# Split weights that move past the transposed input begin 32 bytes into their buffers

## The chip, the cores and the metric

The kernel runs on one core of a Trainium2 chip. Its time is device microseconds of that core for one execution of the whole program; lower is better. TensorE multiplies matrices: one operand of 128 columns is loaded into the array (LDWEIGHTS, the stationary operand) and up to 512 columns of the other move past it (MATMUL). VectorE and ScalarE do elementwise work, GpSimd (POOL) a little, and SyncE (SP) issues the transfers from device memory.

## The reference

A decoder trunk of two layers on a sequence of 256 tokens, model width 1024, all in float32. Each layer is a half-step SwiGLU FFN (inner width 2816), a token-mixing sub-layer, and a second FFN; a final norm follows.

```python
for l in range(DEPTH):
    h = h + 0.5 * swiglu(rms_norm(h, ffn1_norm[l]), ffn1_w_in[l], ffn1_w_out[l])
    u = rms_norm(h, mix_norm[l])
    (z_s, xbc, dt_s, qkv, z_d, b_d, a_d, gate_s, gate_d) = jnp.split(u @ w_in[l], split_points, axis=-1)
    y_s = mamba2_branch(z_s, xbc, dt_s, ...)
    y_d = deltanet_branch(qkv, z_d, b_d, a_d, ...)
    merged = (jax.nn.sigmoid(gate_s) * (y_s @ ssm_w_branch[l])
              + jax.nn.sigmoid(gate_d) * (y_d @ dn_w_branch[l]))
    h = h + merged @ w_out[l]
    h = h + 0.5 * swiglu(rms_norm(h, ffn2_norm[l]), ffn2_w_in[l], ffn2_w_out[l])
return rms_norm(h, final_norm)
```

## The kernel before

A float32 product is made of three products of a shorter format (fp32r): each operand is split into a high part and a low rest, and hi·hi, hi·lo and lo·hi are added in PSUM. The weights come from memory in forms of 128 x 1024 float32 (4096 bytes in each partition), in the order in which they are used. A list, `plan`, holds one entry for each form: its kind, which raw loads it needs, and how many loads must have been issued. `take()` hands out the next form; ahead of it, `load` issues transfers into five buffers `wraw`, and `prep` has ScalarE write the high part (`whi`) and VectorE the rest (`wlo`), into a ring of five buffers each (`NSPL`). Most forms have kind "d"; the kinds "q0" to "q6" are those of a block scheme in the second FFN product, which are also added and subtracted before they are split.

The normalised input is turned by TensorE, split in the same way, and kept in one tile `uT` (high and low part, 8 blocks of 128 input rows, 256 tokens). In the layout of the memory within a partition, `h` (8192 bytes), `cs` (3584), `mhalf` (4, padded to 32), `one` (512) and two tiles `Y` (2048 each) precede `uT`, and it begins at byte 32928, which is 257 x 128 + 32. The ten buffers of `whi` and `wlo` begin at byte 78464 = 613 x 128 and follow each other every 4096 bytes, so each begins on a multiple of 128, as do the tiles `gh`, `gl`, `bh`, `bl`, `mh`, `ml`, `bsa` to `bsd` (split activations) and `wsc`.

Which operand moves differs by place:
- `tok_chunk` (by way of `mm3`): a block of `uT` is stationary and 512 columns of `whi` or `wlo` move. It makes the first chunk of each FFN (PSUM tiles f) and, in the mixer, the z columns and the two gates (PSUM tiles t): 48 matmuls of 512 columns for a chunk of four forms, four chunks f and sixteen chunks t in all.
- `chan_pair` (PSUM tiles fc, the rest of the FFN's first product) and `chan_chunk` (kk, qq, vv, zd, bc, xs in the mixer): a block of the weights is stationary and `uT` moves.
- `out_chunks` and `block_products` (b, o, p): split activations are stationary and the weights move; `uT` isn't used.

In the mixer the string `ORDER` gives the order of the steps: z.. and g.. are token chunks (each name is half a chunk, two forms), k, q, v, d, b, x are channel chunks (two forms), N is the DeltaNet branch product (eight forms); the SSD branch product (16 forms) and the output product (8) follow. A scheduler (Tile) places the instructions of each engine and gives tiles of a pool their buffers in turn; `s2` is a pool of nine buffers of 2048 bytes for short-lived tiles.

Of the kernel before, what the change touches and what calls it, by code (L numbers as in the profile page):

```python
# [7 lines left out]
F32 = mybir.dt.float32  # L8
F32R = mybir.dt.float32r
# [7 lines left out]
P = 128  # L17
# [13 lines left out]
NSPL = 5  # L31
# [12 lines left out]
ORDER = """  # L44
# [7 lines left out]
def trunk_kernel(ctx, tc, x, wst, wsm, norms, lpar, rpar, cst, out):  # L52
# [4 lines left out]
    wpool = ctx.enter_context(tc.tile_pool(name="wpool", bufs=1))  # L57
    slots = ctx.enter_context(tc.tile_pool(name="slots", bufs=1))
    s2 = ctx.enter_context(tc.tile_pool(name="s2", bufs=9))
# [5 lines left out]
    def act(o, i, func=AF.Copy, **kw):  # L65
        return A.activation(out=o, in_=i, func=func, **kw)  # L66

    def tt(o, a, b, op):
        return V.tensor_tensor(out=o, in0=a, in1=b, op=op)  # L69

    def stt(o, a, s, b, op0, op1):
        return V.scalar_tensor_tensor(out=o, in0=a, scalar=s, in1=b, op0=op0, op1=op1)

    def ts(o, a, s1, op0, sc2=None, op1=None):
        if op1 is None:
            return V.tensor_scalar(out=o, in0=a, scalar1=s1, scalar2=None, op0=op0)
        return V.tensor_scalar(out=o, in0=a, scalar1=s1, scalar2=sc2, op0=op0, op1=op1)

    def f(ap):
        return ap.bitcast(F32)  # L80

    def tmp2(name):
        return s2.tile([P, 512], F32, tag="s2", name=name)

    def trb(name):
        return trp.tile([P, 512], F32, tag="tr", name=name)
# [4 lines left out]
    def small(shape, name, bufs=2):  # L91
        return sm.tile(shape, F32, tag=name, name=name, bufs=bufs)
# [3 lines left out]
    mix = (n_dram - 2 * DEPTH * (4 * FC + 22)) // DEPTH  # L96
    plan, stream = [], []

    def plan_plain(j, n):
        for i in range(j, j + n):  # L100
            stream.append(i)
            plan.append(("d", [len(stream) - 1], len(stream)))
        return j + n

    def plan_ffn(j):


        o, j2, held = j + 4 * FC, j + 4 * FC + 22, []
        for kind in FFN:
            if kind in "fc":  # L110
                j = plan_plain(j, 4 if kind == "f" else 2)
            elif kind == "d":
                o = plan_plain(o, 1)
            else:
                if kind == "A":
                    where = [len(stream) + i for i in range(3)]
                    stream.extend(range(o, o + 3))
                    held.append((where, o + 2))
                    o += 4
                    for i, need in enumerate((2, 3, 3, 3)):  # L120
                        plan.append((f"q{i}", where, where[0] + need))
                else:
                    where, b22 = held.pop(0)
                    where += [len(stream) + 1, len(stream)]
                    stream.extend([b22, b22 + 1])
                    for i in range(4, 7):
                        plan.append((f"q{i}", where, len(stream)))
        return j2

    j0 = 0  # L130
    for _ in range(DEPTH):
        j0 = plan_ffn(plan_plain(plan_ffn(j0), mix))
    assert j0 == n_dram
    n_raw = len(stream)
    first = {js[0] for kind, js, _ in plan if kind == "q0"}
# [12 lines left out]

    def prep(i):
        kind, js, _ = plan[i]  # L150
        hi = wpool.tile([P, 1024], F32R, tag="whi", name="whi", bufs=NSPL)
        lo = wpool.tile([P, 1024], F32R, tag="wlo", name="wlo", bufs=NSPL)

        def less(o, a, b):
            tt(raws[js[o]][:], raws[js[a]][:], raws[js[b]][:], ALU.subtract)


        r = raws[js[{"q2": 1, "q4": 4, "q5": 3}.get(kind, 0)]]
        with ExitStack() as behind:
            for ins in state["behind"].pop(i, ()):  # L160
                behind.enter_context(tc.issue_after(ins))
            act(hi[:], r[:])
            if kind == "q1":
                less(1, 2, 1)
            elif kind == "q2":
                less(0, 2, 0)
            elif kind == "q4":
                less(0, 3, 0)
            tt(lo[:], r[:], f(hi[:]), ALU.subtract)
            if kind == "q0":  # L170
                less(0, 1, 0)
        for o in {"d": (0,), "q2": (1,), "q3": (2,), "q4": (4,), "q5": (3,), "q6": (0,)}.get(kind, ()):
            raws.pop(js[o])
        halves[i] = (hi, lo)

# [360 lines left out]
    def mixer(l, nxt):  # L536
# [58 lines left out]
        def scalars():  # L595
            psm = trb("psm")
            for kt in range(KT):
                both = wsc[:, kt].rearrange("p o c -> p (o c)")
                if kt < KT - 1:
                    PE.matmul(psm[0:96, 0:S], both, uTh[:, kt, :], start=kt == 0, stop=False)  # L600
                PE.matmul(psm[0:48, 0:S], wsc[:, kt, 0], uTl[:, kt, :], start=False, stop=False)
                if kt == KT - 1:
                    PE.matmul(psm[0:96, 0:S], both, uTh[:, kt, :], start=False, stop=True)
            smT = s2.tile([96, S], F32, tag="s2", name="smT")
            act(smT[:], psm[0:96, 0:S])
            pst = trb("pst")
            for t in range(2):
                PE.transpose(pst[:, t * 96 : (t + 1) * 96], smT[:, t * P : (t + 1) * P], ident[0:96, 0:96])
            pv2 = pst[:, 0:192].rearrange("p (t o c) -> p t o c", t=2, o=2)
            pvs = small([P, 2, 48], "pvs", 1)  # L610
            pv = pvs[:]
            act(pv, pv2[:, :, 1])
            tt(pv, pv2[:, :, 0], pv, ALU.add)
            scr = s2.tile([P, 5, 2, 40], F32, tag="s2", name="scr")
            xb, ax, z, s_, q_ = (scr[:, i] for i in range(5))
            tt(xb, pv[:, :, 0:40], rp[:, None, 0:40].to_broadcast([P, 2, 40]), ALU.add)
            act(dq[:, :, 8:16], pv[:, :, 40:48], AF.Tanh, scale=0.5)
            ts(dq[:, :, 8:16], dq[:, :, 8:16], 0.5, ALU.mult, 0.5, ALU.add)
            ea = small([P, 40], "ea", 1)
            with tc.issue_after(state["input"][0].ins):  # L620
                act(ea[:], alog, AF.Exp)
            stt(ax, xb, -1.0, xb, ALU.mult, ALU.max)
            act(z, ax, AF.Exp, scale=-1.0)
            ts(s_, z, 2.0, ALU.add)
            V.reciprocal(out=s_, in_=s_)
            tt(s_, s_, z, ALU.mult)
            tt(q_, s_, s_, ALU.mult)
            ts(z, q_, 1.0 / 15.0, ALU.mult)
            for d_ in (13.0, 11.0, 9.0, 7.0, 5.0, 3.0):
                stt(z, z, 1.0 / d_, q_, ALU.add, ALU.mult)  # L630
            stt(z, z, 1.0, s_, ALU.add, ALU.mult)
            ts(ax, xb, 0.0, ALU.max)
            stt(sp[:], z, 2.0, ax, ALU.mult, ALU.add)
            stt(la[:], sp[:], -1.0, ea[:, None, :].to_broadcast([P, 2, 40]), ALU.mult, ALU.mult)
            yield
            psr = trb("psr")
            for t in range(2):
                PE.matmul(psr[0:40, t * 256 : (t + 1) * 256], la[:, t, :], UU, start=True, stop=True)
            pr = psr[:].rearrange("p (t c) -> p t c", t=2)
            V.tensor_copy(rows[0:32], pr[0:32, :, 0:P])  # L640
            V.tensor_copy(rows[32:40], pr[32:40, :, P : 2 * P])
            nc.sync.dma_start(rdram[:], rows[:].rearrange("p t c -> p (t c)"))
            pac = trb("pac")
            for t in range(2):
                PE.transpose(pac[:, t * 40 : (t + 1) * 40], rows[:, t, :], ident[0:40, 0:40])
            V.tensor_copy(ac[:], pac[:, 0:80].rearrange("p (t c) -> p t c", t=2))
            V.tensor_copy(dq[:, :, 0:8], ac[:, :, 32:40])
            yield
            psp = trb("psp")
            for c in range(4):  # L650
                PE.matmul(psp[:, c * 16 : (c + 1) * 16], SEL[c % 2], dq[:, c // 2, :], start=True, stop=True)
            for a in range(2):
                V.tensor_copy(
                    pq[64 * a : 64 * a + 64].rearrange("p k h c -> p c k h"),
                    psp[64 * a : 64 * a + 64, 0:64].rearrange("p (c k h a) -> p c k h a", c=4, k=2, h=4)[:, :, :, :, a],
                )
# [484 lines left out]
        def dn_branch():  # L1141
            ps = branch("d", 4, dn_T)
            m = tg[1]
            for t in range(2):
                for n in range(2):
                    sl = slice(n * 512, (n + 1) * 512)
                    stt(m[:, t, sl], m[:, t, sl], 1.0, ps[t][n][:], ALU.add, ALU.mult)

        sc, inv, rc = scalars(), invert(), recur()
        units = {"k": k_unit, "q": q_unit, "v": v_unit}  # L1150
        rests, heads = {}, {}
# [79 lines left out]
    for t in range(2):  # L1231
        add(t)
        o = [tmp2("fo") for _ in range(2)]
# [141 lines left out]
```

## Time and profile before

| | |
|---|---|
| time, median of 3 runs | 1569.63 us (1569.55 to 1570.59) |
| the profiled execution: its time | 1567.59 us |
| its span, first to last instruction | 1565.8 us |
| granted TensorE clock in it | 0.999 |
| TensorE busy | 1545.0 us (99%) |
| weight loads (beside TensorE's matmuls) | 1342.0 us (86%) |
| VectorE busy | 1302.4 us (83%) |
| ScalarE busy | 999.8 us (64%) |
| transfers | 293 MB, mean 187 GB/s |

Each row of the profile names line, engine, operation, the tile written and the tiles read, the shape and a count. A matmul's time in such a row runs from its start to a modelled end, and successive matmuls overlap; the distance from one start to the next start is what a matmul takes from the engine's time. The chain is followed back from the last instruction, at each step to what released it.

### The profile page before, as it was taken

The page shows a single profiled execution, that of the slowest core. Times are in us where ns is not written, and L with a number is a line of the kernel's source. Part 1 is how long each engine was busy: PE and PEld are TensorE (multiplying, and loading weights), DVE is VectorE, ACT ScalarE, POOL GpSimd, SP SyncE. Part 2 cuts the span into 40 slices and gives each one's busy share as a digit, 9 for nine tenths or more (in the row PEclk, how much of TensorE's full clock was granted, in tenths as well). Part 3 has the DMA queues.
Part 4 walks back from the last instruction along what each step waited for, and adds up shares of the span by engine and source line. Part 5 has one row for each costly group of instructions (what it writes and reads, how often), then busy time and mean ns, then how long its engine had stood idle before and what let it go on. Part 6 is the DMA issues. An engine that isn't in the chain of part 4 may idle for free.

```text
span 1565.8 us, 26672 instructions
## 1 busy us (share of the span) xinstructions
PE 1545.0 (99%) x10152; PEld 1342.0 (86%) x10152; DVE 1302.4 (83%) x2048; ACT 999.8 (64%) x1694; POOL 53.2 (3%) x60
## 2 busy tenths in 40 slices
PE   8999999999999999999999999999999999999998
PEld 6888779999888888888788887899998888888886
DVE  6889969957899766899878998699579996679897
ACT  6666668766675655666566676686656666466664
POOL 0000010000000000000000001010000000000000
PEclk9999999999999999999999999999999999999999
DMA  8565565553455555465765566555336546555553
GB/s 298 197 214 188 195 212 173 178 158 118 174 207 173 177 205 196 159 210 177 262 204 187 168 198 223 189 189 189 116 123 213 177 166 212 201 175 166 198 189 134
DMA packets 94215, 292.99 MB, mean 187 GB/s; under 512 B 22325, under 2 KB 23301, under 8 KB 93062
## 3 DMA queue, kind: packets, MB, share of 16 engines
q1 hardware_dynamic: 94086, 291.29, 55.2%
q8 instruction: 79, 1.29, 0.3%
q14 instruction: 50, 0.41, 0.1%
HBM read 289.33 MB, written 1.92 MB: 186 GB/s over the span
## 4 chain that ended last, share of the span: by engine, by line
PE 76%; DVE 13%; DMA 5%; issue 3%; ACT 2%; POOL 1%; SPq 0%; POOLq 0%; DVEq 0%; ACTq 0%
PE fc L342 15%; PE fc L346 8%; DVE wlo L69 7%; PE t L287 3%; PE t L288 3%; PE t L289 3%; DMA wraw<-in_wst_dram 3%; PE b L289 3%; PE b L288 3%; PE b L287 2%; PE xs L292 2%; PE xs L293 2%; PE xs L294 2%; PE o L288 1%; PE o L289 1%
## 5 line engine op out<-in xcount | busy, mean ns | idle before, releaser
L69 DVE TENSOR_TENSOR wlo<-wraw,whi 128x1024 fp32r<-128x1024 f32 x488 | 591.0, 1221 | 139.8 <-ACT whi L66 136.1
L66 ACT ACTIVATE whi<-wraw 128x1024 fp32r<-128x1024 f32 x488 | 511.6, 1057 | 176.4 <-PE b L289 29.8
L342 PE MATMUL fc<-uT,whi 128*128 128x512 f32 x1280 | 445.5, 391 | 0.0
L346 PE MATMUL fc<-uT,wlo 128*128 128x256 f32 x1280 | 360.9, 282 | 0.0
L342 PEld LDWEIGHTS fc<-uT,whi 128*128 128x128 f32 x1280 | 240.3, 188 | 50.7
L346 PEld LDWEIGHTS fc<-uT,wlo 128*128 128x128 f32 x1280 | 241.8, 189 | 0.8
L287 PE MATMUL t<-whi,uT 128*128 128x512 f32 x256 | 102.9, 403 | 0.0
L288 PE MATMUL t<-wlo,uT 128*128 128x512 f32 x256 | 101.5, 396 | 0.2 <-DVE wlo L69 0.2
L289 PE MATMUL t<-whi,uT 128*128 128x512 f32 x256 | 101.5, 397 | 0.0
L66 ACT ACTIVATE whi<-wfirst 128x1024 fp32r<-128x1024 f32 x64 | 67.8, 1059 | 29.7 <-DVE wfirst L69 20.4
L66 ACT ACTIVATE sg<-fc 128x256 f32<-128x256 f32 x80 | 30.6, 382 | 82.3 <-PE fc L346 82.3
L69 DVE TENSOR_TENSOR wlo<-wfirst,whi 128x1024 fp32r<-128x1024 f32 x64 | 78.1, 1220 | 2.0 <-ACT whi L66 1.9
L287 PE MATMUL b<-whi,bh 128*128 128x512 f32 x192 | 76.1, 398 | 0.0
L288 PE MATMUL b<-wlo,bh 128*128 128x512 f32 x192 | 74.9, 390 | 0.0
L289 PE MATMUL b<-whi,bl 128*128 128x512 f32 x192 | 74.3, 394 | 0.3 <-DVE bl L69 0.3
L292 PE MATMUL xs<-uT,whi 128*128 128x256 f32 x256 | 73.1, 286 | 0.0
L294 PE MATMUL xs<-uT,wlo 128*128 128x256 f32 x256 | 71.6, 280 | 0.0
L293 PE MATMUL xs<-uT,whi 128*128 128x256 f32 x256 | 71.4, 279 | 0.0
L288 PE MATMUL o<-wlo,gh 128*128 128x512 f32 x160 | 64.6, 404 | 2.6 <-DVE wlo L69 2.5
L69 DVE TENSOR_TENSOR wfirst<-wraw,wfirst 128x1024 f32<-128x1024 f32 x48 | 58.6, 1220 | 8.9 <-DMA wraw<-in_wst_dram 8.9
L289 PE MATMUL o<-whi,gl 128*128 128x512 f32 x160 | 62.5, 391 | 0.0
L287 PE MATMUL o<-whi,gh 128*128 128x512 f32 x160 | 62.1, 392 | 0.0
(317 smaller groups left out, 3424.5 us busy)
## 6 DMA issues: line engine op xcount, KB each, us to landing
wraw<-in_wst_dram SPq DMA_DIRECT2D x504, 512.0 KB, 4.5
wfirst<-in_wst_dram SPq DMA_DIRECT2D x16, 512.0 KB, 5.8
dc<-rdram SPq DMA_DIRECT2D x8, 1024.0 KB, 8.4
nw<-in_norms_dram SPq DMA_DIRECT2D x6, 512.0 KB, 6.2
gb<-rdram SPq DMA_DIRECT2D x8, 256.0 KB, 5.3
h<-in_x_dram SPq DMA_DIRECT2D x4, 256.0 KB, 5.7
out_dram<-fo SPq DMA_DIRECT2D x4, 256.0 KB, 2.1
dq<-X SPq DMA_DIRECT2D x2, 256.0 KB, 5.0
```

What stands on the lines that cost most here:

```text
L66: return A.activation(out=o, in_=i, func=func, **kw)
L69: return V.tensor_tensor(out=o, in0=a, in1=b, op=op)
L287: PE.matmul(ps, lh, rh, start=start, stop=False)
L288: PE.matmul(ps, lh, rl, start=False, stop=False)
L289: return PE.matmul(ps, ll, rh, start=False, stop=stop)
L292: PE.matmul(ps, wh, mh, start=start, stop=False)
L293: PE.matmul(ps, wh, ml, start=False, stop=False)
L294: PE.matmul(ps, wl, mh, start=False, stop=stop)
L342: PE.matmul(ps[a][:], wh[:, c0 : c0 + P], uT[:, kt].rearrange("p o t -> p (o t)"), start=kt == 0, stop=False,)
L346: PE.matmul(ps[a][:, 0:S], wl[:, c0 : c0 + P], uTh[:, kt, :], start=False, stop=kt == KT - 1)
```

## The change

The plan gets a kind "t" for forms whose weights move past `uT`: the first FFN chunk, and in the mixer the z and gate forms. A form of this kind is treated as one of kind "d", except that its `whi` and `wlo` are the 1024 columns from column 8 on (32 bytes) of a buffer that is now 1056 columns long. All other forms begin at column 0 as before. The buffers follow each other every 4224 bytes (33 x 128) now. To make room, the small tile `pvs` (384 bytes) moves from a buffer of its own into the ring `s2`.

```diff
+    def plan_mix(j):
+        j1 = plan_plain(j, 4, "t")
+        for name in ORDER:
+            if name[0] in "zg":
+                j1 = plan_plain(j1, 2, "t")
+            elif name[0] in "kqvdbx":
+                j1 = plan_plain(j1, 2)
+            elif name == "N":
+                j1 = plan_plain(j1, 8)
+        j1 = plan_plain(j1, 24)
+        assert j1 == j + mix
+        return j1
...
             if kind in "fc":
-                j = plan_plain(j, 4 if kind == "f" else 2)
+                j = plan_plain(j, 4, "t") if kind == "f" else plan_plain(j, 2)
...
-        j0 = plan_ffn(plan_plain(plan_ffn(j0), mix))
+        j0 = plan_ffn(plan_mix(plan_ffn(j0)))
...
     def prep(i):
         kind, js, _ = plan[i]
-        hi = wpool.tile([P, 1024], F32R, tag="whi", name="whi", bufs=NSPL)
-        lo = wpool.tile([P, 1024], F32R, tag="wlo", name="wlo", bufs=NSPL)
+        c0 = 8 if kind == "t" else 0
+        hi = wpool.tile([P, 1024 + 32], F32R, tag="whi", name="whi", bufs=NSPL)[:, c0 : c0 + 1024]
+        lo = wpool.tile([P, 1024 + 32], F32R, tag="wlo", name="wlo", bufs=NSPL)[:, c0 : c0 + 1024]
...
-            pvs = small([P, 2, 48], "pvs", 1)
+            pvs = s2.tile([P, 2, 48], F32, tag="s2", name="pvs")
```

On every engine the instructions stand in the same order before and after, and all begin behind the same waits, but for two places of SyncE's queue in each layer, where the buffers of `s2` have moved on by one. The first is where the four transfers `gb` (rows of the decay, read back from memory by all partitions) stand between weight loads. Before:

```order
L642 DMA rdram<-rows 40x256 [waits DVE_49]
L146 DMA wraw<-in_wst_dram 128x1024 [waits DMAHW0_49,DVE_49]
L688 DMA gb<-rdram 128x512 [waits DMAHW5_49,PE_49]
L688 DMA gb<-rdram 128x512 [waits PE_49]
L688 DMA gb<-rdram 128x512 [waits DMAHW1_49]
L688 DMA gb<-rdram 128x512 [waits DMAHW2_49]
```

The same place of SyncE's queue after:

```order
L657 DMA rdram<-rows 40x256 [waits DVE_49]
L160 DMA wraw<-in_wst_dram 128x1024 [waits DMAHW0_49,DVE_49]
L703 DMA gb<-rdram 128x512 [waits DMAHW5_49,PE_49]
L703 DMA gb<-rdram 128x512
L703 DMA gb<-rdram 128x512 [waits DMAHW1_49]
L703 DMA gb<-rdram 128x512 [waits DMAHW2_49,PE_49]
```

The second transfer has lost its wait for TensorE and the fourth has got one, for the transposes `hnT` of the norm's second token block. The second place is the transfer `X` some thirty rows later, which now waits for the transposes into `pst` as well.

More of the change, by code (lines that the diff above doesn't have):

```diff
@@ L97, in trunk_kernel, with plan_plain @@
     plan, stream = [], []
-    def plan_plain(j, n):
+    def plan_plain(j, n, kind="d"):
         for i in range(j, j + n):
             stream.append(i)
-            plan.append(("d", [len(stream) - 1], len(stream)))
+            plan.append((kind, [len(stream) - 1], len(stream)))
         return j + n
+    def plan_mix(j):
[10 more added lines that the diff above has]
+        return j1
     def plan_ffn(j):
@@ L171, in prep @@
                 less(0, 1, 0)
-        for o in {"d": (0,), "q2": (1,), "q3": (2,), "q4": (4,), "q5": (3,), "q6": (0,)}.get(kind, ()):
+        for o in {"d": (0,), "t": (0,), "q2": (1,), "q3": (2,), "q4": (4,), "q5": (3,), "q6": (0,)}.get(kind, ()):
             raws.pop(js[o])
```

## The prediction

> **What bounds the kernel now.** I read the page first: busy shares, clock, and the chain that ended last.
>
> ```profile
> PE 1545.0 (99%) x10152; PEld 1342.0 (86%) x10152; DVE 1302.4 (83%) x2048; ACT 999.8 (64%) x1694; POOL 53.2 (3%) x60
> PEclk9999999999999999999999999999999999999999
> PE 76%; DVE 13%; DMA 5%; issue 3%; ACT 2%; POOL 1%; SPq 0%; POOLq 0%; DVEq 0%; ACTq 0%
> ```
>
> TensorE holds 76% of the chain at a full granted clock, so what a matmul costs from its start to the next one's start is most of the time. The change alters the addresses of one operand, so the question is whether that distance depends on addresses. The view of a tile's instructions (minimum/median/maximum in ns) sets matmuls of one shape and dtype, 512 moving columns, beside each other (PEld is the load of the stationary operand):
>
> ```profile
> L288 PEld LDWEIGHTS t<-wlo,uT x256: 186/188/192, 193.1 to 1302.7; 128*128 128x128 f32 x128
> L288 PE MATMUL t<-wlo,uT x256: 392/395/501, 193.3 to 1303.0; 128*128 128x512 f32 x128
> L288 PE MATMUL f<-wlo,uT x64: 392/396/794, 10.3 to 1391.3; 128*128 128x512 f32 x64
> L288 PEld LDWEIGHTS b<-wlo,bh x192: 187/188/192, 467.6 to 1353.8; 128*128 128x128 f32 x192
> L288 PE MATMUL b<-wlo,bh x192: 387/389/402, 467.8 to 1354.0; 128*128 128x512 f32 x192
> L288 PE MATMUL p<-wlo,bsa x48: 389/389/389, 70.8 to 1496.9; 128*128 128x512 f32 x48
> L288 PE MATMUL o<-wlo,gh x160: 387/389/504, 159.3 to 1558.5; 128*128 128x512 f32 x160
> L342 PE MATMUL fc<-uT,whi x1280: 390/390/484, 24.4 to 1524.7; 128*128 128x512 f32 x183
> ```
>
> In t and f the stationary operand is the transposed input uT, which begins 32 bytes behind a multiple of 128, and a split weight whi or wlo moves, which begins on one: 395 to 396. In b, p and o both begin on a multiple of 128: 389. In fc the roles are turned, uT moves: 390. Ends are modelled, so I check with starts, in the timeline: one run of t (48 matmuls, first and last), one of p (18), one of fc (16 pairs of a 512- and a 256-column matmul), each with the row that follows it.
>
> ```profile
> 439.06 0.40 PE L287 MATMUL t<-whi,uT 128*128 128x512 f32 x1
> ...
> 450.03 0.40 PE L289 MATMUL t<-whi,uT 128*128 128x512 f32 x1
> 450.27 0.82 PE L1045 MATMUL xsb<-cs,xsT 128*128 128x128 f32 x6
> ```
>
> ```profile
> 70.61 0.39 PE L287 MATMUL p<-whi,bsa 128*128 128x512 f32 x1
> ...
> 74.46 0.39 PE L289 MATMUL p<-whi,bsa 128*128 128x512 f32 x1
> 74.69 0.40 PE L342 MATMUL fc<-uT,whi 128*128 128x512 f32 x1
> ```
>
> ```profile
> 24.42 0.39 PE L342 MATMUL fc<-uT,whi 128*128 128x512 f32 x1
> ...
> 29.85 0.28 PE L346 MATMUL fc<-uT,wlo 128*128 128x256 f32 x1
> 29.96 0.38 PE L514 MATMUL gT<-cs,sg 128*128 128x128 f32 x2
> ```
>
> t: (450.27 − 439.06) / 48 = 233.5 ns. p: (74.69 − 70.61) / 18 = 226.7 ns. fc: 5.54 / 16 = 346.3 ns a pair, against 1.5 × 226.7 = 340.0. So t and f pay 6.8 ns more a matmul than p, with the same columns, the same clock and no wait.
>
> **The change part by part.** *The offset.* It moves the operand of 256 × 3 t and 64 × 3 f matmuls, 960 in all; no instruction is added and none changes its place on any engine. What of them lies on the path is read from the chain: over the whole span for t, in the stretch of each first FFN chunk for f.
>
> ```profile
> by line: PE fc L342 15.5%; PE fc L346 8.2%; DVE wlo L69 6.9%; PE t L287 3.4%; PE t L288 3.4%; PE t L289 3.4%; DMA wraw<-in_wst_dram 2.9%; issue 2.7%; PE b L289 2.6%; PE b L288 2.5%; PE b L287 2.5%; PE xs L292 1.6%; PE xs L293 1.6%; PE xs L2
> by line: DMA h<-in_x_dram 55.9%; PE f L289 16.6%; PE f L287 15.4%; PE f L288 15.2%; ACT junk L66 9.1%; PE hnT L254 6.9%; DVE hn L72 4.9%; POOL zz L189 3.7%; issue 1.8%; DVE zz L77 1.5%
> by line: PE f L289 19.6%; PE f L287 17.9%; PE f L288 17.9%; DVE wlo L69 12.4%; DVE h L72 9.9%; PE hnT L254 8.2%; issue 6.1%; DVE hn L72 5.9%; POOL zz L189 4.4%; DVE zz L77 1.1%
> ```
>
> t: 10.2% of 1565.8 = 159.7 us. f: 47.2% of the 15.42 us from 9 to 24.42, and 55.4% of the 13.04 us from 603.8 to 616.84; I count the other two chunks like the second: 7.3 + 3 × 7.2 = 28.9 us. Together 188.6 us, at 233.5 ns some 808 matmuls. The other 150 lie behind a norm or a transfer that is late anyway; faster, they only wait longer. The largest such place is the first t chunk of layer 0, where the chain goes through a transfer instead:
>
> ```profile
> 199.00 6.39 DMA wsr<-in_wsm_dram
> ```
>
> The price of a matmul with both operands 32 bytes behind stands in no row. Best end: as p, 226.7, so 6.8 saved on all 960, 6.5 us. Worst end: each operand that starts off a multiple pays for itself, and t keeps its 233.5 and adds what fc pays: 6.3 ns a pair is 4.2 per 512 columns, on 808 matmuls 3.4 us more. I take 228.0: the two cases of unequal offsets, t and fc, are dearer than the equal one, which speaks for the difference between the operands and not for either start, and b, which stands among transposes like t, is a little above p:
>
> ```profile
> 532.55 0.39 PE L289 MATMUL b<-whi,bl 128*128 128x512 f32 x1
> ...
> 537.33 0.39 PE L289 MATMUL b<-whi,bl 128*128 128x512 f32 x1
> 537.57 0.60 PE L1113 MATMUL yT<-cs,yz 128*128 128x128 f32 x4
> ```
>
> That is 5.02 / 22 = 228.2. So 5.5 × 808 = −4.4 us.
>
> *What is late next.* After the gate chunk at 439 VectorE has hardly a gap, and the chain leaves TensorE at 455.66:
>
> ```profile
> 443.73 1.23 DVE L69 TENSOR_TENSOR wlo<-wraw,whi 128x1024 fp32r<-128x1024 f32 x1 [0.60 <-ACT whi L66]
> ...
> 455.95 0.68 DVE L69 TENSOR_TENSOR xe<-xdt,dE 128x512 f32<-128x512 f32 x1
> 456.75 1.23 DVE L69 TENSOR_TENSOR wlo<-wraw,whi 128x1024 fp32r<-128x1024 f32 x1
> ```
>
> VectorE is free there at 456.63, 0.12 us before the split that it waits for, and the 90 chain matmuls since 414 (two gate chunks, 42 and 48) save 0.5. Part of that moves the run that began at 443.73 too, since that split waited for ScalarE and this for TensorE; I lose 0.2 us in each layer, an estimate between 0 and 0.4: +0.4.
>
> *The writes.* ScalarE and VectorE now write whi and wlo 32 bytes in. The nearest rows write uT (32 behind) and mh, ml (on a multiple) from PSUM in the same shape:
>
> ```profile
> L66 ACT ACTIVATE uT<-hnT 128x512 fp32r<-128x512 f32 x24 | 13.7, 596 | 14.2 <-PE hnT L254 13.8
> L66 ACT ACTIVATE mh<-mT 128x512 fp32r<-128x512 f32 x8 | 4.6, 594 | 6.0 <-PE mT L1208 6.0
> L69 DVE TENSOR_TENSOR uT<-hnT,uT 128x512 fp32r<-128x512 f32 x24 | 15.4, 682 | 0.0
> L69 DVE TENSOR_TENSOR ml<-mT,mh 128x512 fp32r<-128x512 f32 x8 | 5.5, 686 | 0.1
> ```
>
> 596 to 594 and 682 to 686: nothing either way, within 4 ns × 144 splits = 0.6 us, most of it beside TensorE.
>
> *pvs and the two DMA waits.* pvs takes a turn in the ring of nine s2 buffers. One gb transfer in each layer now waits for the last transposes of the norm, the X transfer for the transposes into pst; behind them on SP's queue stand weight loads. Both are long done:
>
> ```profile
> 198.72 0.60 PE L254 MATMUL hnT<-cs,hn 128*128 128x128 f32 x4
> 214.84 0.33 PE L608 MATMUL pst<-cs,smT 96*128 96x96 f32 x2
> L688 SPq DMA_DIRECT2D gb<-rdram x8: 326/423/1447, 230.7 to 1006.8; - x8
> L816 SPq DMA_DIRECT2D X<-dq x2: 338/338/338, 295.4 to 1071.2; - x2
> ```
>
> 199.3 is 31 us ahead of the first gb, 215.2 is 80 us ahead of X: zero; the added semaphore instruction on SP costs zero too, since loads stand several buffers ahead.
>
> Sum: −4.4 + 0.4 = −4.0 us. The profiled execution took 1567.59 us (span 1565.8) and would take 1563.6; the median of the runs is 2.04 above it, so 1565.6 there. Faster or slower means 0.2%, 3.1 us, about what a measurement of this kernel can tell from no change.
>
> **The rivals.** *The start itself costs, not the difference.* For it: fc, whose moving operand begins 32 behind, is dearer than p. Against: the weight load is as long in t as in b (188), so an offset weight load is not slower by itself. It gives between the 1 ns of fc's 390 over 389 (0.8 us) and 3.4 us more: 1570.4 to 1573.0. In its mildest form neither matters in this place and t is dearer for another reason, such as its neighbours: 1569.6. The Trainium skill, "TensorE: Matmul & The Clock Gate", Part 2, step 1, says that the moving operand and the weight load have read ports of their own and that loading the next weights takes nothing from the running matmul; by it nothing would change. The trace does not agree: 395 against 389 at one shape has no other cause that I see.
>
> *VectorE takes half of it.* Were every t chunk like the one at 439, some 2.2 us would stay: 1567.4. Against it: the chain runs through some 684 of the 768 t matmuls (159.7 us at 233.5 ns).
>
> *128 is not the period: slower.* The buffers also grow from 4096 to 4224 bytes, so whi and wlo now begin at four different places modulo 512, where all were alike. If the cost of a pair of operands goes by 256 or 512, the b, p and o matmuls lose their equal start. It decides if the b rows leave 389. Price: b is 7.6% of the chain, 119 us or 520 matmuls, and I take 430 of p and o with it (six rows like that of p are 288; of the 480 in three rows like that of o a third, since there the splits are late); three quarters of 950 by 6.1 ns are +4.4, while t keeps a quarter of its gain, −1.1: 1572.9. Against it: the weights wsc begin 384 bytes apart, so at all four places modulo 512, and their matmuls with uT vary as little as those with whi:
>
> ```profile
> L600 PE MATMUL psm<-uT,wsc x14: 278/280/281, 212.3 to 988.6; 128*96 128x256 f32 x14
> L293 PE MATMUL xs<-uT,whi x256: 277/279/282, 380.3 to 1276.9; 128*128 128x256 f32 x128
> ```
>
> But these have 256 columns, where little can be told.
>
> **How the numbers follow.** The difference counts and t falls to between 226.7 and 229: 0.62, 1563.2 to 1566.9, of which 0.02 are too small to tell. VectorE takes half: 0.08, no change that can be told. The start itself or nothing: 0.19, of which 0.02 slower. The other period: 0.11, of which 0.10 slower. So faster 0.60, same 0.28, slower 0.12. The range from 1563.2 to 1570.9 leaves out the other period, the upper part of the start's own cost and a little of the best end.
>
> **What would show it.** The t and f medians fall from 395 to 389 or 390, a gate chunk of 48 takes 10.9 to 11.0 us in place of 11.21, and b, o, p, fc stay. Should t read 396 or 397, the start itself costs; should b or p rise, the period is another. Should t fall and the time not, the gap between xe and wlo at 456 is gone and the b matmuls after it start later against the gate chunk. I am wrong above all if t differs from p by what surrounds it and not by addresses.

## The result: slower by 0.56%, and the profile after

The changed kernel takes 1579.19 us (median; 1577.66 to 1581.43), the kernel before 1569.93 us beside it: a ratio of 1.0056, with a 95% interval of 1.0041 to 1.0071. The forecast was 1565.6 us. The profiled execution took 1578.31 us with a span of 1576.5 us at a granted clock of 0.999, so it is 10.7 us longer than the span before. In the changed kernel `mm3` stands at L302 to L304 (before: L287 to L289), fc at L357 and L361 (L342, L346), the channel chunks at L307 to L309 (L292 to L294).

The page of the changed kernel, with busy shares, clock and chain by engine:

```profile
PE 1556.3 (99%) x10152; PEld 1345.2 (85%) x10152; DVE 1303.5 (83%) x2048; ACT 1001.4 (64%) x1694; POOL 53.2 (3%) x60
PEclk9999999999999999999999999999999999999999
PE 82%; DVE 9%; DMA 4%; issue 2%; ACT 2%; POOL 0%; SPq 0%; POOLq 0%; ACTq 0%; DVEq 0%
```

TensorE is busy 11.3 us longer with the same 10152 instructions and the same clock, and its share of the chain rises from 76% to 82%. VectorE, ScalarE and GpSimd are as before. So matmuls themselves have become dearer. Which ones is seen in the view of a tile's instructions (minimum/median/maximum of one, ns), in the changed kernel:

```profile
L303 PE MATMUL t<-wlo,uT x256: 387/393/505, 196.2 to 1310.9; 128*128 128x512 f32 x128
L357 PE MATMUL fc<-uT,whi x1280: 390/394/484, 25.9 to 1534.7; 128*128 128x512 f32 x183
L303 PE MATMUL b<-wlo,bh x192: 388/392/398, 471.2 to 1362.3; 128*128 128x512 f32 x192
L303 PE MATMUL p<-wlo,bsa x48: 390/395/397, 72.9 to 1506.6; 128*128 128x512 f32 x48
L303 PE MATMUL o<-wlo,gh x160: 388/395/505, 162.3 to 1569.2; 128*128 128x512 f32 x160
L308 PE MATMUL xs<-uT,whi x256: 277/281/284, 384.4 to 1285.0; 128*128 128x256 f32 x128
```

By the medians, t has fallen by 2 ns, from 395 to 393, where 389 or 390 was forecast. p and o rise from 389 to 395, b from 389 to 392, fc from 390 to 394, the 256-column xs from 279 to 281. Ends are modelled; starts tell it better. The same three runs that the prediction measured, in the timeline of the changed kernel (gate chunk t, then p, then fc):

```profile
442.46 0.40 PE L302 MATMUL t<-whi,uT 128*128 128x512 f32 x1
...
453.56 0.82 PE L1060 MATMUL xsb<-cs,xsT 128*128 128x128 f32 x6
...
72.65 0.40 PE L302 MATMUL p<-whi,bsa 128*128 128x512 f32 x1
...
76.83 0.39 PE L357 MATMUL fc<-uT,whi 128*128 128x512 f32 x1
...
25.90 0.39 PE L357 MATMUL fc<-uT,whi 128*128 128x512 f32 x1
...
31.52 0.60 PE L529 MATMUL gT<-cs,sg 128*128 128x128 f32 x4
```

t: 11.10 / 48 = 231.3 ns (before 233.5). p: 4.18 / 18 = 232.2 ns (before 226.7). fc: 5.62 / 16 = 351.3 ns a pair (before 346.3). There is a small gain on t and a loss on the other two.

### The profile page after: what moved, and what is told of

The parts are those of the page before. It is cut to its first block, busy times and chain, and to the rows that moved or that the text cites. A ratio compares the mean times of both kernels' runs of the same rounds, so it can differ in the third digit from the quotient of the medians.

```text
span 1576.5 us, 26674 instructions
## 1 busy us (share of the span) xinstructions
PE 1556.3 (99%) x10152; PEld 1345.2 (85%) x10152; DVE 1303.5 (83%) x2048; ACT 1001.4 (64%) x1694; POOL 53.2 (3%) x60
## 4 chain that ended last, share of the span: by engine, by line
PE 82%; DVE 9%; DMA 4%; issue 2%; ACT 2%; POOL 0%; SPq 0%; POOLq 0%; ACTq 0%; DVEq 0%
PE fc L357 17%; PE fc L361 9%; DVE wlo L69 5%; PE t L303 3%; PE t L302 3%; PE t L304 3%; PE b L304 3%; PE b L303 3%; PE b L302 3%; DMA wraw<-in_wst_dram 2%; PE xs L308 2%; PE xs L307 2%; PE xs L309 2%; PE p L302 2%; PE p L303 2%
## 5 line engine op out<-in xcount | busy, mean ns | idle before, releaser
L69 DVE TENSOR_TENSOR wlo<-wraw,whi 128x1024 fp32r<-128x1024 f32 x488 | 590.9, 1221 | 145.3 <-ACT whi L66 143.0
L66 ACT ACTIVATE whi<-wraw 128x1024 fp32r<-128x1024 f32 x488 | 512.7, 1057 | 180.5 <-PE b L304 28.5
L357 PE MATMUL fc<-uT,whi 128*128 128x512 f32 x1280 | 450.0, 395 | 0.0
L361 PE MATMUL fc<-uT,wlo 128*128 128x256 f32 x1280 | 359.2, 281 | 0.0
L357 PEld LDWEIGHTS fc<-uT,whi 128*128 128x128 f32 x1280 | 240.4, 188 | 56.7
L361 PEld LDWEIGHTS fc<-uT,wlo 128*128 128x128 f32 x1280 | 241.1, 188 | 0.9
L302 PE MATMUL t<-whi,uT 128*128 128x512 f32 x256 | 102.5, 402 | 0.0
L304 PE MATMUL t<-whi,uT 128*128 128x512 f32 x256 | 100.7, 394 | 0.0
L302 PE MATMUL b<-whi,bh 128*128 128x512 f32 x192 | 76.6, 401 | 0.0
L304 PE MATMUL b<-whi,bl 128*128 128x512 f32 x192 | 74.6, 395 | 0.3 <-DVE bl L69 0.3
L307 PE MATMUL xs<-uT,whi 128*128 128x256 f32 x256 | 73.6, 287 | 0.0
L309 PE MATMUL xs<-uT,wlo 128*128 128x256 f32 x256 | 72.2, 282 | 0.0
L304 PE MATMUL o<-whi,gl 128*128 128x512 f32 x160 | 62.7, 392 | 0.0
L302 PE MATMUL o<-whi,gh 128*128 128x512 f32 x160 | 62.5, 395 | 0.0
```

The lines of the kernel that those rows point to most:

```text
L302: PE.matmul(ps, lh, rh, start=start, stop=False)
L304: return PE.matmul(ps, ll, rh, start=False, stop=stop)
L307: PE.matmul(ps, wh, mh, start=start, stop=False)
L309: PE.matmul(ps, wl, mh, start=False, stop=stop)
L357: PE.matmul(ps[a][:], wh[:, c0 : c0 + P], uT[:, kt].rearrange("p o t -> p (o t)"), start=kt == 0, stop=False,)
L361: PE.matmul(ps[a][:, 0:S], wl[:, c0 : c0 + P], uTh[:, kt, :], start=False, stop=kt == KT - 1)
```

## The experiments

Below, a "distance" is the mean time from one matmul's start to the next one's, in ns, worked out from the trace over all places in the profiled execution where two matmuls in fp32r follow each other. Distances above 300 ns (150 ns for 256 columns) are left out as waits; stretches at half the granted clock drop out with them. A column is named after the PSUM tile and the number of columns that move, so fc512 + fc256 is the time of a pair. The column xs256 is that of xs alone; the other five kinds of channel chunks (some 2,600 matmuls with xs) lie within 1 to 2 ns of it. All twelve experiments and the two kernels, with the ratio of their time to that of the kernel before:

```
                          t512   fc512  fc256   b512   o512   p512   xs256   ratio to before [95%]
before                   233.1   228.6  118.3  228.0  227.9  227.3   116.7
after                    231.2   232.5  117.9  230.8  231.2  231.5   118.5   1.0056 [1.0041, 1.0071]
spacing_alone            233.2   232.5  117.9  230.5  231.1  231.5   118.7   1.0070 [1.0053, 1.0086]
offset_alone             227.9   236.4  116.8  233.2  233.2  233.1   119.8   1.0102 [1.0087, 1.0118]
input_on_128             227.8   235.7  116.8  228.0  228.0  228.2   119.9   1.0060 [1.0043, 1.0076]
hi_lo_4096               230.4   230.2  117.8  231.1  231.4  232.2   117.3   1.0049 [1.0031, 1.0067]
places_equal_512         227.6   228.6  118.3  228.1  228.0  227.3   116.9   1.0010 [1.0002, 1.0018]
places_two_of_256        227.8   228.6  118.3  228.2  227.9  227.3   116.9   1.0006 [0.9997, 1.0014]
pair_before              233.2   228.6  118.3  227.9  228.1  227.3   117.0   1.0036 [1.0023, 1.0050]
spacing_4352             227.9   228.6  118.3  228.0  228.0  227.2   116.7   0.9983 [0.9973, 0.9993]
spacing_4352_no_offset   233.2   228.6  118.3  228.0  228.0  227.3   116.7   0.9997 [0.9987, 1.0006]
weights_128_later        233.4   229.4  117.5  232.4  232.5  232.4   118.2   1.0053 [1.0037, 1.0070]
input_at_64              233.3   231.0  119.1  228.2  228.1  227.7   116.9   1.0037 [1.0022, 1.0051]
input_at_96              234.1   232.2  117.9  227.9  228.0  228.0   120.0   1.0074 [1.0057, 1.0092]
```

It helps to have the places modulo 256 of the kernel before at hand: the split weights and the split activations begin at 128, `uT` at 160. So b, o and p have equal starts there, and those of t, fc and the chunks are 32 bytes apart.

**The spacing without the offset.** The buffers 4224 bytes apart as in the changed kernel, every form at column 0:

```diff
-        c0 = 8 if kind == "t" else 0
+        c0 = 0
```

> The changed kernel with all split weights at column 0: the buffers stay 4224 bytes apart and pvs stays in s2, the 32 bytes are gone. Theory S (the spacing costs: whi and wlo at several places modulo 512): as slow as the changed kernel or slower, 1579 to 1582 us, with fc at 232 to 233 ns from start to start, b, o and p at 231, the 256-column chunks at 118.3, and t back at 233 or above. Theory O (the 32-byte start costs, by its reads or its writes): back to 1568 to 1571 us, fc at 228.6, b and p at 227 to 228.

Measured 1581.63 us (1579.14 to 1583.27). The whole loss is there without any offset: t is back at 233.2, and all other distances are those of the changed kernel to within 0.3 ns. So by the distances the 32 bytes gained a little on t, and the longer buffers lost more elsewhere. The times of the two kernels are not told apart (1.0070 and 1.0056, and the intervals overlap).

**The offset without the spacing.** The kernel before, with all ten weight buffers begun 32 bytes later (a small tile ahead of them, another behind them, so that all other tiles keep their places modulo 1024):

```diff
+        wpool.tile([P, 8], F32, tag="pad", name="pad", bufs=1)
         hi = wpool.tile([P, 1024], F32R, tag="whi", name="whi", bufs=NSPL)
         lo = wpool.tile([P, 1024], F32R, tag="wlo", name="wlo", bufs=NSPL)
+        wpool.tile([P, 248], F32, tag="pad2", name="pad2", bufs=1)
```

> The kernel before with a gap of 32 bytes ahead of all whi and wlo buffers, which stay 4096 bytes apart; every split weight begins 32 behind a multiple of 128, as uT does, and the other tiles keep their places modulo 1024. Theory S with an equal start: t and f fall from 233 to 227 ns, the fc pair from 346 to 340, the 256-column chunks from 117 to 114, while b, o and p, now unequal, rise from 227 to between 229 and 233; 1552 to 1566 us. Theory O: t and f stay at 233 or rise, and with them fc and the rest: 1570 us or more.

Measured 1586.66 us (1585.57 to 1587.47). t falls to 227.9, the full gain that was forecast (228.0). b, o and p, now 32 bytes away from their stationary operands, rise to 233, as t was. But fc and the channel chunks, whose two operands now begin alike modulo 256, do not gain: fc rises from 228.6 to 236.4 and xs from 116.7 to 119.8.

**uT on a multiple of 128.** The kernel before, with `uT` allocated earlier, so that it begins at byte 28288 = 221 x 128:

```diff
+    uT = cpool.tile([P, KT, 2, S], F32R, name="uT")
     mhalf = ...
...
-    uT = cpool.tile([P, KT, 2, S], F32R, name="uT")
```

> The kernel before with uT allocated ahead of three small tiles, so that it begins on a multiple of 128 (at 640 modulo 1024, as the weights); nothing else moves that matmuls of the weights read. Theory S with an equal start: t and f 227 ns (-4 us), fc pairs 340 in place of 346 (-8), 256-column chunks 114 in place of 117 (-8 to -9), b, o, p unchanged: 1546 to 1556 us. If equal starts count only for a stationary uT: 1565 to 1566 us with fc and the chunks unchanged. If starts don't count (t is dear by its surroundings): 1569 to 1571 us.

Measured 1580.29 us (1578.74 to 1581.4). It is the same equality by the other way, without touching the weights: t 227.8, b, o and p unchanged, fc 235.7 and xs 119.9. The view of a tile's instructions for this kernel:

```profile
L288 PE MATMUL t<-wlo,uT x256: 387/389/501, 196.5 to 1314.5; 128*128 128x512 f32 x128
L342 PE MATMUL fc<-uT,whi x1280: 389/398/477, 26.1 to 1538.1; 128*128 128x512 f32 x183
L293 PE MATMUL xs<-uT,whi x256: 278/283/288, 385.0 to 1288.9; 128*128 128x256 f32 x128
```

t reads 389 like b and p, fc 398 in place of 390, xs 283 in place of 279. So equal starts are the cheapest tried for the matmuls in which 512 columns of the weights move, and among the dearest tried for those in which `uT` moves. The rule "equal is good" does not carry over when the roles are turned.

**The high and the low part 4096 bytes apart.** The changed kernel, with whi and wlo of a form in one buffer of 8320 bytes:

```diff
-        hi = wpool.tile([P, 1024 + 32], F32R, tag="whi", name="whi", bufs=NSPL)[:, c0 : c0 + 1024]
-        lo = wpool.tile([P, 1024 + 32], F32R, tag="wlo", name="wlo", bufs=NSPL)[:, c0 : c0 + 1024]
+        both_ = wpool.tile([P, 2048 + 32], F32R, tag="whl", name="whl", bufs=NSPL)
+        hi, lo = both_[:, c0 : c0 + 1024], both_[:, c0 + 1024 : c0 + 2048]
```

> The changed kernel with whi and wlo of a form in one buffer of 2080 columns, 4096 bytes apart; the five buffers are 8320 bytes apart, so their places modulo 1024 still differ by 128 from one to the next. Theory S1 (what costs is the step from the high to the low operand, 128 modulo 256 in the changed kernel and 0 before): t near 227 to 228 ns, fc 228 to 229, b and p 227: 1564 to 1568 us. Theory S2 (what costs is the place of a buffer against the other operand modulo 256 or more): fc, b and p stay at 230 to 233, with forms of even and of odd buffers apart: 1574 to 1580 us.

Measured 1578.31 us (1575.2 to 1581.03), not told apart from the changed kernel. fc and xs come back by more than half, b, o and p not at all. The pairs themselves still follow each other by 128 modulo 256. The run changes one thing more: five pairs of 8320 bytes end 640 bytes later than the ten buffers of the kernel before, so by the order of the pools the split activations behind them have moved by 128 modulo 256 too. The two are not separated here. The pair also has a price of its own, shown below, which is in this time.

**All weights of a kind alike modulo 512, and modulo 256.** The changed kernel with its offset, pairs of 8704 bytes (17 x 512), and then of 8448 bytes (33 x 256). Room is made by putting two more small tiles (`one`, `rows`) into rings that have space:

```diff
+        both_ = wpool.tile([P, 2048 + 128], F32R, tag="whl", name="whl", bufs=NSPL)
...
-    one = cpool.tile([1, P], F32, name="one")
+    one = slots.tile([1, P], F32, tag="y1", name="one")
...
-        rows = sm.tile([40, 2, P], F32, tag="rows", name="rows", bufs=1)
+            rows = s2.tile([40, 2, P], F32, tag="s2", name="rows")
```

> The changed kernel with its 32-byte offset for the forms of kind t, but with each whi and wlo in one buffer of 8704 bytes, 4096 apart, so that all weights of a kind begin at one place modulo 512 (128 for d and q, 160 for t), as gh, bh and bsa do. Theory (the offset did what the prediction said, and the four places modulo 512 were the cost): t and f fall to 228 ns from start to start, b, o and p stay at 227 to 228, fc at 228.6 and 118.3 ns, the 256-column chunks at 117; in all 1563 to 1567 us, median 1565. Rival (the place modulo 1024, still of two kinds here, or a pair in one buffer, is what costs): b, o and p stay at 231 or above, 1570 to 1577 us.

> As places_equal_512, but the pairs follow each other every 8448 bytes, so that the places are alike modulo 256 and of two kinds modulo 512. If the period is 256: as places_equal_512, t, b, o, p at 228 ns, about 1565 us. If it is 512: b, o and p at 229 to 232, about 1570 to 1576 us.

Measured 1571.99 us (1569.81 to 1575.07) and 1571.45 us (1569.88 to 1573.16). In both every distance is at its best: t 227.6 and 227.8, and all others as in the kernel before. Two places modulo 512 cost nothing, so the period is not 512. It is not 128 either: buffers 4224 apart are alike modulo 128 and were dear. That leaves 256. Yet the time did not follow. The expectation held for the distances and missed the time by 6 to 7 us.

**Where the gain went: the pair.** The timeline of VectorE around the chain's bend at 410 us, in the kernel before and then in places_two_of_256 (start, duration, line, operation; in brackets the idle time before and what ended it):

```profile
406.59 1.23 DVE L69 TENSOR_TENSOR wlo<-wraw,whi 128x1024 fp32r<-128x1024 f32 x1 [0.87 <-ACT whi L66]
407.98 1.23 DVE L69 TENSOR_TENSOR wlo<-wraw,whi 128x1024 fp32r<-128x1024 f32 x1 [0.17 <-ACT whi L66]
410.41 2.29 DVE L69 TENSOR_TENSOR dc<-dc,ac 128x2048 f32<-128x2048 f32 x1 [1.20 <-DMA dc<-rdram]
412.62 0.68 DVE L69 TENSOR_TENSOR vb<-ob,os 128x512 f32<-128x512 f32 x1
```

```profile
410.00 2.29 DVE L69 TENSOR_TENSOR dc<-dc,ac 128x2048 f32<-128x2048 f32 x1 [4.38 <-DMA dc<-rdram]
412.21 2.35 DVE L69 TENSOR_TENSOR whl<-wraw,whl 128x1024 fp32r<-128x1024 f32 x2
414.48 0.69 DVE L69 TENSOR_TENSOR vb<-ob,os 128x512 f32<-128x512 f32 x1
```

With one buffer for both parts the scheduler places two splits behind `dc` instead of ahead of it. `dc` waits for a transfer until 410 in both; VectorE idles 4.38 us with the splits queued behind it, and `vb`, for which the chain waits, starts 1.9 us later. TensorE waits for `vb` ahead of its matmuls `cbb`: 2.38 us here and again 2.38 us at the same place of the second layer, against 1.03 and 0.58 us in the kernel before. That is 3.2 us more in all. To test it alone, the kernel before with nothing but the pair, 4096 and 8192 bytes apart, every place modulo 1024 as it was:

```diff
-        hi = wpool.tile([P, 1024], F32R, tag="whi", name="whi", bufs=NSPL)
-        lo = wpool.tile([P, 1024], F32R, tag="wlo", name="wlo", bufs=NSPL)
+        both_ = wpool.tile([P, 2048], F32R, tag="whl", name="whl", bufs=NSPL)
+        hi, lo = both_[:, :1024], both_[:, 1024:]
```

> The kernel before with each whi and wlo in one buffer of 8192 bytes, all places alike modulo 1024 as before. Every distance between matmuls as in before (t 233, b 228, fc 228.6). Theory (the pair makes the scheduler put dc, which waits for a transfer, ahead of two splits and vb on VectorE, 4 us in each layer): 1574 to 1579 us. Rival (the pair costs nothing): 1569 to 1571 us.

Measured 1576.3 us (1573.81 to 1578.17) against 1570.9 us: 5.4 us for the pair (3.6 to 7.9 by the interval of the ratio), with every distance of the table as before. Its VectorE stands as in places_two_of_256:

```profile
410.70 2.29 DVE L69 TENSOR_TENSOR dc<-dc,ac 128x2048 f32<-128x2048 f32 x1 [4.80 <-DMA dc<-rdram]
412.91 2.35 DVE L69 TENSOR_TENSOR whl<-wraw,whl 128x1024 fp32r<-128x1024 f32 x2
415.18 0.69 DVE L69 TENSOR_TENSOR vb<-ob,os 128x512 f32<-128x512 f32 x1
```

But the order is not all of it. The matmuls `cbb` that follow `vb`, in the kernel before, in places_two_of_256 and in pair_before:

```profile
413.36 0.70 PE L989 MATMUL cbb<-BC 128*128 128x256 f32 x2 [1.03 <-DVE vb L69]
...
415.22 0.70 PE L1004 MATMUL cbb<-BC 128*128 128x256 f32 x2 [2.38 <-DVE vb L69]
...
415.92 1.22 PE L989 MATMUL cbb<-BC 128*128 128x256 f32 x2 [2.79 <-DVE vb L69]
```

In the last the same two matmuls take 1.22 us in place of 0.70: behind the 2.79 us of idle time the granted clock is 0.50 from 416 to 419 us, and behind 3.15 us of idle time in the second layer it is 0.50 from 1195 to 1200 us. In places_two_of_256 it stays at 1.00 behind both waits of 2.38 us. Halved clocks thus cost this profiled run, at 1578.17 us the slowest of its five, some 4 us (an estimate: half of the 8 us, in which TensorE is busy throughout). The waits alone cost less than 5.4 us: places_two_of_256 and spacing_4352 (below) have the same distances and differ by the pair, and their medians are 3.7 us apart (those of the kernel before beside them 0.4). So the expected 4 us in each layer fell within the range with half of the cause unseen.

**Separate buffers, 4352 bytes apart, with and without the offset.** The changed kernel with 1088 columns (17 x 256 bytes) for each buffer, no pair; the small tiles `one` and `rows` moved as above:

```diff
-        hi = wpool.tile([P, 1024 + 32], F32R, tag="whi", name="whi", bufs=NSPL)[:, c0 : c0 + 1024]
-        lo = wpool.tile([P, 1024 + 32], F32R, tag="wlo", name="wlo", bufs=NSPL)[:, c0 : c0 + 1024]
+        hi = wpool.tile([P, 1024 + 64], F32R, tag="whi", name="whi", bufs=NSPL)[:, c0 : c0 + 1024]
+        lo = wpool.tile([P, 1024 + 64], F32R, tag="wlo", name="wlo", bufs=NSPL)[:, c0 : c0 + 1024]
```

> The changed kernel with buffers of 1088 columns (4352 bytes, 17 x 256) for whi and wlo each, so that all weights of a kind begin at one place modulo 256 and the 32-byte offset of the t forms is kept. Theory (the spacing is the fault of the change; pairs in one buffer lost their gain because the two splits stand behind dc on VectorE's queue, and here they stand ahead of it as before): t and f 228 ns, b, o, p 228, fc 228.6 and 118.3, chunks 117, vb after t at 412.5 us as before; 1563.5 to 1567.5 us, median 1566. Rival (the gain of t is lost to VectorE and the transfers wherever it arises): the same distances, but 1569 to 1572 us, no change.

> As spacing_4352, but all forms begin at column 0 of their buffers. Theory: all as in the kernel before, t at 233 ns, the room made elsewhere costs nothing: 1569 to 1571 us; so spacing_4352 is 4 to 5 us faster than this one. Rival: the two differ by less than 2 us.

With the offset 1567.74 us (1564.77 to 1571.28), without it 1570.62 us (1568.42 to 1572.35), the kernel before 1570.9 us. So the offset is worth 2.9 us between the medians of twelve runs each, and 3.8 us between the profiled spans (1565.1 and 1568.9), somewhat less than the 4 to 5 us expected. The moved tiles and the longer buffers cost nothing that can be told (0.9997, interval 0.9987 to 1.0006). The first of the two beats both kernels of this study: 0.9983 of the time before (0.9973 to 0.9993). Page, tile view and the gate chunk in the timeline, of spacing_4352:

```profile
PE 1542.1 (99%) x10152; PEld 1342.5 (86%) x10152; DVE 1302.6 (83%) x2048; ACT 999.1 (64%) x1694; POOL 53.2 (3%) x60
...
L303 PE MATMUL t<-wlo,uT x256: 387/389/504, 193.8 to 1301.3; 128*128 128x512 f32 x128
...
437.91 0.40 PE L302 MATMUL t<-whi,uT 128*128 128x512 f32 x1
...
448.80 0.82 PE L1060 MATMUL xsb<-cs,xsT 128*128 128x128 f32 x6
```

The 48 matmuls take 10.89 us, 226.9 ns each, as short as p.

**All weights 128 bytes later.** The kernel before, with the weights still alike among themselves; only their distance to the other operands changes, by 128. The edit is that of the second experiment with 32 and 224 columns in place of 8 and 248.

> The kernel before with all ten weight buffers begun 128 bytes later, still 4096 apart, and all other tiles at their places modulo 1024. Theory A (what counts is the distance between the two operands of a matmul modulo 256): b, o and p, now 128 apart modulo 256, rise from 228 to 231 or 233 ns, fc and the chunks change too: 1575 to 1583 us. Theory B (what counts is that the weights are spread over several places modulo 256; a common shift by 128 does nothing): b, o, p 228, t 233, fc 228.6, 1569.5 to 1571.5 us.

Measured 1577.62 us (1572.12 to 1581.07). b, o and p rise to 232.4 to 232.5; the run of p in the timeline of this kernel:

```profile
71.39 0.40 PE L289 MATMUL p<-whi,bsa 128*128 128x512 f32 x1
...
75.58 0.39 PE L344 MATMUL fc<-uT,whi 128*128 128x512 f32 x1
```

That is 4.19 / 18 = 232.8 ns against 226.7. Theory A holds: with nothing spread, a distance of 128 bytes modulo 256 between a matmul's two operands costs b, o and p 4.4 to 5.1 ns. What spread adds is not settled. Sorting the o matmuls of the changed kernel by their form's place in the ring (a reconstruction from the plan, with the five `whi` ahead of the five `wlo`) gives about 230 ns where the next matmul's weights lie at the same place modulo 256, whether the matmul's own operands are alike (84 of them) or 128 apart (40), and 231 to 232 where the next one's lie at the other place (some 590). None of these reaches 228. So more than a matmul's own two operands has a part there; a change of place from one moving operand to the next may be it, which no run here tests alone.

**uT 64 and 96 bytes behind.** The kernel before with `uT` 32 or 64 bytes later, weights untouched (the edit for 64; for 96 the two pads have 16 and 240 columns):

```diff
+    cpool.tile([P, 8], F32, name="pad")
     uT = cpool.tile([P, KT, 2, S], F32R, name="uT")
+    cpool.tile([P, 248], F32, name="pad2")
```

> The kernel before with uT begun 32 bytes later, 64 behind a multiple of 128; every weight stays on a multiple of 128, 4096 bytes apart, and b, o and p keep their operands. b, o, p 227 to 228 ns. If what matters is whether the two starts are equal modulo 128: t at 233 and fc at 228.6 and 118 as before, 1569.6 us, the same. If it matters how far apart they are: t above 233 or fc and the chunks off their values of before by 1 ns or more; by 1 ns in all of them 960 x 1 + 1280 x 2 + 1400 x 1, 5 us either way.

> The kernel before with uT begun 64 bytes later, 96 behind a multiple of 128, weights as before. If the distance counts without its sign, 96 is 32 the other way round and all is as before: t 233, fc 228.6 and 118, 1569.6 us. If the sign counts: fc and the chunks change by 1 ns or more, 3 us or more in all. As in input_at_64, t at 233 if only equality modulo 128 counts.

Measured 1576.59 us (1573.98 to 1578.13) and 1581.6 us (1580.55 to 1584.93). t stays at 233 to 234 for every unequal place; fc and the chunks change from place to place. With a period of 256, what mirrors 32 is 224, which was not tried. What mirrors 96 is 160, and so far behind the weights `uT` begins in weights_128_later: there xs takes 118.2 and a pair fc 346.9, at 96 they take 120.0 and 350.1. So the sign counts, or the places themselves do. The kernel before already had the best place tried for fc and the chunks, at 32 bytes, and one of the dear ones for t.

## Why the prediction was wrong

*The offset, term −4.4 us: right, but only where the spacing is a multiple of 256.* t was forecast at 228.0 and takes 227.9 in spacing_4352, 227.9 in offset_alone and 227.8 in input_on_128. That both operands begin equally far behind counts for t, and not either start alone: three kernels with the start of one or the other moved show it. The rival that the start itself costs is refuted. In the changed kernel t reaches 231.2 only.

*Late next, +0.4 us: not contradicted.* The gap that the prediction named, between xe and the split behind it at 456, is 0.12 us in spacing_4352 too, as it was (timeline of VectorE in that kernel):

```profile
455.02 0.68 DVE L69 TENSOR_TENSOR xe<-xdt,dE 128x512 f32<-128x512 f32 x1
455.82 1.23 DVE L69 TENSOR_TENSOR wlo<-wraw,whi 128x1024 fp32r<-128x1024 f32 x1
```

The distances gave 768 x 5.3 + 192 x 5.1 = 5.1 us (t and f, against spacing_4352_no_offset; f, which the table leaves out, falls from 233.5 to 228.4), the spans 3.8 us and the medians 2.9 us. The sum of −4.0 lies between these; how much of the rest is lost behind VectorE was not measured by itself.

*Writes, pvs, the two waits, 0 us: right.* ScalarE's and VectorE's splits take 1057 and 1221 ns in the page before and in the page after:

```profile
L69 DVE TENSOR_TENSOR wlo<-wraw,whi 128x1024 fp32r<-128x1024 f32 x488 | 591.0, 1221 | 139.8 <-ACT whi L66 136.1
L66 ACT ACTIVATE whi<-wraw 128x1024 fp32r<-128x1024 f32 x488 | 511.6, 1057 | 176.4 <-PE b L289 29.8
...
L69 DVE TENSOR_TENSOR wlo<-wraw,whi 128x1024 fp32r<-128x1024 f32 x488 | 590.9, 1221 | 145.3 <-ACT whi L66 143.0
L66 ACT ACTIVATE whi<-wraw 128x1024 fp32r<-128x1024 f32 x488 | 512.7, 1057 | 180.5 <-PE b L304 28.5
```

pvs and its two waits are in spacing_4352_no_offset, with the two other moved tiles, and nothing is lost there.

*The step that failed: the spacing of the buffers, taken as free in the sum and priced as a rival at +3.3 us with a chance of 0.11.* The change has it as a side effect: 4224 is 16 x 256 + 128, so the ten buffers lie at two places modulo 256. This rival had the cause right (the cost of a pair of operands goes by more than 128, and b, o and p lose 4.4 to 5.1 ns with their equal start in weights_128_later; how that adds up where the weights are spread stays open, as said above). It was mis-sized and badly rejected:

- It counted b, o and p alone. From the table's rows for before and after, and the number of distances: b, o and p 532 x 2.8 + 707 x 3.3 + 384 x 4.2 = 5.4 us, where the rival had 4.4. fc 1276 x (3.9 − 0.4) = 4.5 us and the channel chunks some 2600 x 1.5 = 3.9 us were not in it at all. t and f give back 724 x 1.9 + 171 x 1.2 = 1.6 us. Together 12.2 us, against 11.3 us more of TensorE's busy time and 10.7 us more span.
- The rows set against it, psm and xs, could not carry that. psm, with weights at all four places modulo 512, stays at 117.3 to 118 from start to start in all but two of the kernels, also where xs of the same 256 columns goes from 116.7 to 118.5 or 120, so it does not tell what xs pays. The whole effect on xs is 1.8 of 116.7 ns by the starts and 2 ns by the medians (279 to 281), no more than the spread within each of the two rows compared.

*A second false step, that did not decide here:* fc, dear by 6.3 ns a pair, was read as a case of "unequal is dearer" beside t. The two experiments that make fc's operands equal show the opposite: 352.5 and 353.2 ns a pair in place of 346.9. What holds for one pattern (`uT` stationary, 512 columns of the weights moving) had been taken for a law of the address. The forecast of 228.0 for t leant on fc as one of its two cases and came out all the same; that part of it was luck.

The Trainium skill, "SBUF — State Buffer", section "SBUF: two separate sides", says that on the engines' side only the port pair shared by GpSimd and VectorE brings contention, and that TensorE never waits on anyone. That is about engines waiting for each other. Here the places of TensorE's own two operands have a price: p takes 227.3 ns before and 232.4 in weights_128_later, at the same shape and the same granted clock of 0.999, with only addresses changed. What inside the chip makes it so, no run here shows.

## What to carry to other kernels

A buffer that is made longer moves every buffer behind it: before a change of addresses, write down each operand's place modulo 128, 256 and 512 before and after, and price all matmuls whose places change, not only those that the change is for. In this kernel spacings of a multiple of 256 cost nothing; keep to them and change the place of one operand of one kind of matmul, and check the kinds in which the same tile plays the other role, since their best place may be another. Measure such effects from start to start over a run of matmuls, and compare the order on VectorE, and the granted clock in each stretch, when two tiles are merged into one: the merge alone cost 5.4 us here, part of it by a halved clock that a mean of 0.996 hides.

## What the runs showed of the hardware that was not expected

- Two fp32r matmuls of 512 columns in a row, with a full clock and no wait, are 227 to 228 ns apart when both operands begin alike modulo 256 (p, b and o before, t in spacing_4352), 232.4 when they are 128 apart (p, b and o in weights_128_later), and 233 to 234 when they are 32, 64 or 96 apart (t before, in input_at_64 and in input_at_96). No reason was found.
- Where a 512- and a 256-column matmul with the same moving tile alternate (fc), a pair takes 346.9 ns when the moving operand begins 32 bytes behind the stationary one modulo 256 (the kernel before), 350.1 at 64 and at 96, and 352.5 to 353.2 at 0 (input_on_128, offset_alone). For a matmul of the 256-column chunks (xs) it is 116.7 at 32, 116.9 at 64, 120.0 at 96 and 119.8 to 119.9 at 0. Why the best place differs from that of t was not found.
- Weights 4352 bytes apart (two places modulo 512) cost the same as weights 4096 apart, weights 4224 apart cost more: the period seen is 256 bytes.
- The granted clock fell to 0.50 behind TensorE's idle stretches of 2.79 and 3.15 us (pair_before) and 3.09 us (places_equal_512, second layer, 0.50 from 1192 to 1194.5 us), and stayed at 1.00 behind two of 2.38 us (places_two_of_256) and one of 2.29 us (places_equal_512, first layer).
